# Attention values as products with tokens stationary and 512 weight columns moving

## Chip, cores and metric

The kernel runs on one core of a Trainium2 chip. The metric is the device time of one execution in microseconds (us). The engines are TensorE (PE, with its weight loads shown apart as PEld), VectorE (DVE), ScalarE (ACT), GpSimd (POOL) and SyncE (SP); each works through its own instructions in the order of the program, and DMA transfers are started from the queues of SP and POOL. In this kernel SP starts the loads of weights, and POOL starts the loads of attention's tables and the stores of keys and values.

## The reference, cut to what matters

Two layers of a block work on 128 context tokens and 256 latent tokens. Of one layer, what the change touches is this:

```
u = h @ w_in
u_pool, u_q, u_k, u_v, u_x, u_y, u_g = jnp.split(u, SPLITS, axis=-1)
q = u_q.reshape(b, l, N_HEADS, HEAD_DIM)
k = u_k.reshape(b, l, N_HEADS, HEAD_DIM)
v = u_v.reshape(b, l, N_HEADS, HEAD_DIM)
y_b = attn_fn(q, k, v).reshape(b, l, ATTN_W)
...
s_lat = einsum('brqhd,brkhd->bhrqk', qg, kb) * ATTN_SCALE + bias
s_ctx = einsum('brqhd,bkhd->bhrqk', qg, ck) * ATTN_SCALE
p = softmax(concatenate([s_lat, s_ctx], axis=-1), axis=-1)
o = einsum('bhrqk,brkhd->brqhd', p_lat, vb) + einsum('bhrqk,bkhd->brqhd', p_ctx, cv)
```

The width of h is 1024; there are 8 heads of 64, so u_v is 512 wide. The values v of the context tokens are also an output of the kernel (new_cache_v). Attention mixes tokens, so it needs v with tokens on the partitions, while everything else in the kernel has features on the partitions and tokens in the free dimension.

## The kernel before

All 384 tokens go through the layer together. A product of the main stream is a job (the function of that name): a chunk of weights, 8 blocks of 128 by 128, is stationary, the 384 tokens move, and each block takes three matmuls, since weights and data are split into an exact high and a low half (`whi`, `wlo`; `hh`, `hl`; L341 to L343). So a job of one chunk is 24 matmuls into one bank of PSUM. The order of the chunks is written out in chunk_order; SP loads them ahead, ACT makes the high half (L304) and DVE the low half (L313).

Other work stands beside the main stream. After the matmuls of a job the program traces, in this order: one step of each evacuation that is under way (tick), one step of each side branch (side_step), the evacuation of the job itself (push), and some steps of modulation on DVE (after). The side branches are Python generators; what a step traces goes to the engines' programs at that place, so the order of the engines' work follows the order of the jobs.

The part that the change touches begins behind the gates of the recurrent branch. Two side branches are then started: branch_lru_scan, whose steps scan one chunk of channels in one direction on DVE (L655) and copy one column of state to `st` on POOL (L656), and branch_attn. The main stream goes through four pairs of heads; for each pair p, qkv(p) traces

- load_attn: four DMAs on POOL for the tables `bias` of the two heads (L679) and one for `ckv`, the cached keys and values of the pair (L682);
- a job for q, one for k and one for v of the pair; each is copied from PSUM by ACT (L857), and k and v go out by a DMA on POOL (L859).

branch_attn works in steps i = 0, 1, 2 and so on, one at each side_step, and starts with pair p once `v` of that pair is there. Step 4p begins the pair (begin): PE transposes three blocks of v (L764), which ACT copies back to SBUF as `vv` a step later (L796), and DVE adds the mask to the two bias tables (L688). Then the scores of the pair's first query tile follow on PE (L701): q is stationary, and k and the cached keys in `ckv` move. Later steps take the softmax, transpose the probabilities (L743) and multiply them with `vv` and `ckv` (L778, L783).

After the twelve jobs the main stream goes on with the gates and projections of branch 2 (the recurrent one), 16 jobs with a step of attention at each, and then of branch 1 (attention's own), before which all side work must have been traced.

Of the kernel before, what the change touches and what calls it, by code (L numbers as in the profile page):

```python
# [16 lines left out]
L = 2  # L17
# [28 lines left out]
# products that warm the tensor engine up, around the first modulation vectors  # L46
WN = (8, 1, 1)
# modulation steps for each group of products, by part of the layer
# [3 lines left out]
def chunk_order():  # L52
    o = []
    for l in range(L):
        ms = [0, 1, 2, 3, 16, 17, 18, 19, 20, 21, 22, 23]
        if l == 0:
            ms = [m for m in ms if m not in FIRST0]
        o += [("in", l, m, 8) for m in ms]
        o += [("pw", l, 0, 4)]
        for b in (0, 2, 1):  # L60
            o += [("in", l, 24 + b * 8, 8)]
            for d in range(8):
                if b == 0 and d in (2, 6):
                    o += [("lru", l, d // 4, 8)]
                if d < 7:
                    o += [("in", l, 25 + b * 8 + d, 8)]
                o += [("br", l, b * 8 + d, 4)]
            if b == 0:
                for p in range(4):
                    o += [("in", l, 4 + p, 8), ("in", l, 8 + p, 8), ("in", l, 12 + p, 8)]  # L70
        o += [("wo", l, d, 8) for d in range(8)]
        for i in range(KF):
            o += [("fi", l, 2 * i, 8), ("fi", l, 2 * i + 1, 8)]
        for d in range(8):
            o += [("fo", l, 3 * d, 8), ("fo", l, 3 * d + 1, 8), ("fo", l, 3 * d + 2, 6)]
    return o
# [13 lines left out]
def emit(ctx, tc, A, outs):  # L90
# [33 lines left out]
    # silu(c), features on partitions, as the stationary side of small products  # L124
# [13 lines left out]
    # sel[p, s] = 1 where p = s modulo 32  # L138
# [3 lines left out]
    # 2h / count at the clipped ends of the pooling windows  # L142
    edge = cp.tile([128, 4, 2, 8], F32, name="edge")

    # additive mask of key columns, last column first
    cmask = cp.tile([128, 64], F32, name="cmask")

    def build_consts():
        ti = small("ti")
        G.iota(ti, pattern=[[1, 8]], base=0, channel_multiplier=0, allow_small_or_imprecise_dtypes=True)  # L150
        for g in range(4):
            h = float(1 << g)
            V.tensor_scalar(edge[:, g, 0], ti, h, None, op0=OP.add)
            V.tensor_scalar(edge[:, g, 1], ti, -1.0, 2 * h - 1, op0=OP.mult, op1=OP.add)
            yield
        V.tensor_scalar(edge[:, :, 1], edge[:, :, 1], 1.0, None, op0=OP.max)
        yield
        V.reciprocal(edge, edge)
        yield
        for g in range(4):  # L160
            V.tensor_scalar(edge[:, g], edge[:, g], 2.0 * (1 << g), None, op0=OP.mult)
            yield
        G.memset(cmask, 0.0)
        for rr in range(2):
            v = cmask[rr * 64:(rr + 1) * 64]
            # query column p, key column c = 63 - i: c >= min(p - 8, 48) and c < max(p - 8, 0) + 16
            G.affine_select(v[:, 16:64], v[:, 16:64], pattern=[[-1, 48]], base=55,
                            channel_multiplier=-1, compare_op=OP.is_ge, fill=NEG)
            G.affine_select(v[:, 0:48], v[:, 0:48], pattern=[[1, 48]], base=-56,
                            channel_multiplier=1, compare_op=OP.is_ge, fill=NEG)  # L170

    # derived per-channel parameters, both layers at once
# [3 lines left out]
    def build_dpar():  # L176
# [5 lines left out]
        # -log_sigmoid(lam) = max(-lam, 0) + log1p(z), z = exp(-|lam|)  # L182
# [13 lines left out]
        # log1p(z) = 2 atanh(z / (2 + z)), s <= 1/3  # L196
# [28 lines left out]
    def load_crow():  # L225
        # silu(c) * 2, broadcast over partitions
        Q.dma_start(out=crow, in_=A["crow"].unsqueeze(0).to_broadcast([128, 2, D]))
# [102 lines left out]
    def w_ahead(done, full=False):  # L330
        """traced before the products with the last `done` chunks, which still hold their tiles"""
        n = ws["use"] + NH - done
        w_lo(min(ws["cv"], n))
        w_hi(n)
        if full or done > 2:
            w_lo(n if full or done > 3 else n - 1)
        w_dma(min(n + NR, ws["lo"] + NR))
# [7 lines left out]
    def split_from(src, n=NT, scale=1.0, name="s"):  # L345
        """float32 data in SBUF or PSUM (times scale) -> two float32r tiles"""
        hi, lo = heap(name + "h", F32R), heap(name + "l", F32R)
        S.activation(hi[:, :n], src, AF.Copy, scale=scale)
        if isinstance(scale, float) and scale == 1.0:
            V.tensor_tensor(lo[:, :n], src, hi[:, :n].bitcast(F32), op=OP.subtract)  # L350
        else:
            V.scalar_tensor_tensor(lo[:, :n], src, scale, hi[:, :n].bitcast(F32), op0=OP.mult, op1=OP.subtract)
        return hi, lo

    def split_g(put, src, n=NT, scale=1.0, name="s"):
        """split_from in two stages"""
# [50 lines left out]
    def job(mems, mv, evac, units=1.0, full=False):  # L407
        """mems: lists of chunks, one PSUM bank for each; k outermost where there are several"""
# [25 lines left out]
    def prep_x(l, which, d, shift=True):  # L434
        """x * g (1 + sc), not yet divided by the token's rms, with the shift as two more columns"""
# [56 lines left out]
    def normed(l, which, R, mv):  # L492
        """hi and lo of h = rmsnorm(x) * g * (1 + sc) + sh, a pair of tiles per block of features"""
# [36 lines left out]
    def first_group(l, which, keys, evs, kst):  # L530
        """the first products behind a norm: from x before the division, which the evacuation makes up for"""
# [22 lines left out]
    def seg_copy(dst, offs, src):  # L554
        """PSUM (or the pair that undo gives) to the two token ranges of a padded tile"""
# [7 lines left out]
    def branch_pool(l, g, up, y):  # L563
        h = 1 << g
        st = heap("ws")
        # sliding sum over [t - h, t + h)
# [36 lines left out]
    def lru_gates(l, c, w, y):  # L603
        """one chunk of channels, both directions"""
        q = dpar[l]
        xc, mv = y.pop(("xc", c))
        for e in range(2):
# [4 lines left out]
            def ev(pa, px, i, e):  # L612
# [5 lines left out]
                # log a = C (1 + th)  # L618
# [4 lines left out]
                V.scalar_tensor_tensor(t2[:, n], th[:, n], 1.0, t2[:, n], op0=OP.add, op1=OP.mult)       # 1 - a  # L623
                V.scalar_tensor_tensor(th[:, n], t2[:, n], 2.0, t2[:, n], op0=OP.subtract, op1=OP.mult)  # a^2 - 1
                yield
                S.activation(t2[:, n], t2[:, n], AF.Identity, scale=-1.0, bias=1.0)                      # a
# [43 lines left out]
    def load_attn(l, y, p):  # L670
        for h in (2 * p, 2 * p + 1):
            t = heap("bias")
            rpb = A["rpb"]
            for rr in range(2):
                lo = 5 - rr
                # the table's last axis comes reversed; key columns are laid out from the last to the first
# [13 lines left out]
    def branch_attn(l, y):  # L690
        def scores(p, qt):
            """both heads of a pair side by side, each on its half of the rows"""
# [64 lines left out]
        pr, o, tv, pend = {}, {}, {}, []  # L757
        nu = len(units)

        def begin(p):  # L760
            tp = psum("tp")
            vt = y["v", p]
            for j in range(3):
                T.transpose(tp[:, j * 128:(j + 1) * 128], vt[:, j * 128:(j + 1) * 128], ident)  # L764
            tv[p] = tp
            mask_bias(y, p)
# [20 lines left out]
        while i < nu + 7 or pend:  # L787
            if i < nu and ("v", units[i][0]) not in y:
                yield
                continue  # L790
# [3 lines left out]
            for p in list(tv):  # L794
                vv = heap("vv")
                S.activation(vv[:, :384], tv.pop(p)[:, :384], AF.Copy)  # L796
                y["vv", p] = vv
# [18 lines left out]
            if i % 4 == 2 and 0 <= i - 10 < nu:  # L816
# [3 lines left out]
                for key in (("vv", p), ("ckv", p), ("bias", 2 * p), ("bias", 2 * p + 1), ("q", p), ("k", p), ("v", p)):  # L820
                    y.pop(key)
# [32 lines left out]
    def ev_qkv(l, kind, p, y):  # L854
# [8 lines left out]
        return f  # L863

# [66 lines left out]
    def start(y):  # L931
        """modulation of the first norm on the tensor engine, beside the first products; its shift comes last"""
# [27 lines left out]
        def first_mod():  # L960
            """the first scales, one block of features at a time"""
# [76 lines left out]
        def warm(n):  # L1038
            """products of no use that keep the tensor engine's clock up while the first data comes"""
# [126 lines left out]
    for l in range(L):  # L1166
# [14 lines left out]
        def qkv(p):  # L1181
# [3 lines left out]
            win(12 + p, ev_qkv(l, "v", p, y))  # L1185
# [7 lines left out]
        for bi, b in enumerate((0, 2, 1)):  # L1193
# [17 lines left out]
            if b == 0:  # L1211
# [7 lines left out]
                modr[0] = MR[l][3]  # L1219
                for p in range(4):  # L1220
                    qkv(p)
# [31 lines left out]
    # the last norm, tokens on partitions  # L1253
# [24 lines left out]
def layout(i):  # L1278
# [7 lines left out]
    def fm(a):  # [..., n*128] -> [128, ...*n]  # L1286
# [13 lines left out]
    def tiles(w):  # [L, K, M] -> [L, M/128, 128(k), K/128, 128(m)]  # L1300
# [4 lines left out]
    # the first products and their modulation, in the order of their use  # L1305
# [3 lines left out]
    A["in0"] = c(w0.transpose(3, 0, 2, 1, 4).reshape(8, 2, 128, 384))  # L1309
    A["pw"] = c(f["pool_w"].transpose(0, 2, 1, 3).reshape(L, 1, 128, 4, 128))  # L1310
# [40 lines left out]
```

## Time and profile before

| | |
|---|---|
| median of 3 runs | 1251.04 us |
| lowest and highest of the runs | 1250.4 and 1251.63 us |
| span of the profiled execution (its own time, from the first to the last instruction) | 1250.2 us |
| PE busy, share of the span | 99% |
| DVE, ACT, POOL busy, share of the span | 71%, 48%, 6% |

The span is that of one execution that the profiler took; the runs are timed without it, and their median is 0.84 us above this span. A view of the trace gives, for an engine, what it did and when, and what ended the idle time before it.

### The profile page before, as it was taken

The numbers are of one execution on the slowest core, as the hardware profiler recorded it, in microseconds if no ns is written. First come the engines' busy times: TensorE is split into PE (matmuls) and PEld (weight loads), VectorE is DVE, ScalarE is ACT, GpSimd is POOL, SyncE is SP. The second block draws the span as 40 slices with busy tenths as digits, with TensorE's granted clock in tenths as the row PEclk, the third lists the DMA queues.
The fourth block names the chain that finished last, engine by engine and source line by source line (L and its number), as shares of the span: only waits on it lengthen the run. The fifth ranks groups of instructions, "written<-read, shape, count | busy, mean of one in ns | idle before, by whom it ended". The sixth has DMA issues, their size and how long they took to land.

```text
span 1250.2 us, 19496 instructions
## 1 busy us (share of the span) xinstructions
PE 1237.8 (99%) x7414; PEld 1213.4 (97%) x7414; DVE 888.6 (71%) x1650; ACT 599.8 (48%) x1095; POOL 73.0 (6%) x187
## 2 busy tenths in 40 slices
PE   8999999999999999999999999999999999999997
PEld 7799999999999999999999999999999999999997
DVE  5788798988977987756779668975676784442432
ACT  4487765534456333333347577553344743332331
POOL 0000141000200000010000013200010000000000
PEclk8999999999999999999999999999999999999999
DMA  9646676456645666646643557733554365333421
GB/s 330 239 127 211 173 146 155 142 188 209 208 129 172 237 229 206 208 137 191 210 147 103 159 168 171 143 111 118 169 186 135 116 205 168 132 108 103 121 78 51
DMA packets 65438, 204.32 MB, mean 163 GB/s; under 512 B 7744, under 2 KB 12992, under 8 KB 65216
## 3 DMA queue, kind: packets, MB, share of 16 engines
q1 hardware_dynamic: 62848, 197.82, 48.6%
q0 software_dynamic: 2496, 5.25, 4.0%
q8 instruction: 58, 0.95, 0.3%
q14 instruction: 36, 0.29, 0.1%
HBM read 200.41 MB, written 2.63 MB: 162 GB/s over the span
## 4 chain that ended last, share of the span: by engine, by line
PE 73%; issue 22%; DVE 3%; ACT 1%; DMA 0%; SPq 0%; POOLq 0%; POOL 0%; DVEq 0%
PE ps L341 23%; PE ps L343 22%; PE ps L342 22%; PE tp L743 1%; PE sc L701 1%; PE o L783 1%; DVE wlo L313 1%; PE ma L954 1%; DMA w<-in_wm 0%; PE fb L1144 0%; DVE hf L655 0%; ACT th L634 0%; DVE ti L648 0%; PE o L778 0%; ACT whi L304 0%
## 5 line engine op out<-in xcount | busy, mean ns | idle before, releaser
L341 PE MATMUL ps<-hh,whi 128*128 128x384 f32 x1320 | 447.3, 339 | 0.0
L343 PE MATMUL ps<-hl,whi 128*128 128x384 f32 x1320 | 444.5, 337 | 0.0
L342 PE MATMUL ps<-hh,wlo 128*128 128x384 f32 x1320 | 444.3, 337 | 0.0
L313 DVE TENSOR_TENSOR wlo<-raw,whi 128x1024 fp32r<-128x1024 f32 (+2 forms) x296 | 322.4, 1114 | 22.8 <-ACT whi L304 22.8
L304 ACT ACTIVATE whi<-raw 128x1024 fp32r<-128x1024 f32 (+2 forms) x296 | 280.1, 970 | 102.9 <-PE ps L343 62.0
L341 PEld LDWEIGHTS ps<-hh,whi 128*128 128x128 f32 x1320 | 247.8, 188 | 1.6 <-issue 0.3
L343 PEld LDWEIGHTS ps<-hl,whi 128*128 128x128 f32 x1320 | 247.8, 188 | 0.0
L342 PEld LDWEIGHTS ps<-hh,wlo 128*128 128x128 f32 x1320 | 247.8, 188 | 0.0
L261 DVE SCALAR_TENSOR_TENSOR junk<-wm,crow 128x1024 bf16<-128x1024 f32 x160 | 195.2, 1220 | 26.3 <-DMA wm<-in_wm 24.2
L343 PE MATMUL ps<-svl,whi 128*128 128x384 f32 x352 | 118.7, 337 | 0.0
L341 PE MATMUL ps<-svh,whi 128*128 128x384 f32 x352 | 118.6, 337 | 0.0
L905 ACT ACTIVATE ft<-ps 128x384 f32<-128x384 f32 x40 | 19.7, 492 | 206.0 <-PE ps L343 206.0
L342 PE MATMUL ps<-svh,wlo 128*128 128x384 f32 x352 | 118.3, 336 | 0.0
L890 DVE SCALAR_TENSOR_TENSOR x<-ps,modv,x 128x128 f32<-128x128 f32 x64 | 23.7, 411 | 85.2 <-PE ps L343 85.0
L907 DVE TENSOR_TENSOR ft<-ft,ps 128x384 f32<-128x384 f32 x40 | 22.0, 551 | 84.2 <-ACT ft L905 66.7
L868 ACT ACTIVATE tg<-ps 128x384 f32<-128x384 f32 x48 | 23.5, 489 | 114.5 <-PE ps L343 114.5
L343 PEld LDWEIGHTS ps<-svl,whi 128*128 128x128 f32 x352 | 66.1, 188 | 0.0
L341 PEld LDWEIGHTS ps<-svh,whi 128*128 128x128 f32 x352 | 66.1, 188 | 0.0
L342 PEld LDWEIGHTS ps<-svh,wlo 128*128 128x128 f32 x352 | 66.1, 188 | 0.0
L877 DVE SCALAR_TENSOR_TENSOR tg<-tg,ps 128x384 f32<-128x384 f32 x48 | 26.5, 551 | 53.5 <-PE ps L343 53.0
L452 ACT ACTIVATE sq<-x 128x384 f32<-128x384 f32 x40 | 20.1, 513 | 67.4 <-DVE x L890 67.4
L342 PE MATMUL ps<-mgh,wlo 128*128 128x384 f32 x128 | 43.2, 338 | 0.0
(239 smaller groups left out, 1713.0 us busy)
## 6 DMA issues: line engine op xcount, KB each, us to landing
raw<-in_in SPq DMA_DIRECT2D x90, 512.0 KB, 4.2
raw<-in_fi SPq DMA_DIRECT2D x88, 512.0 KB, 4.3
wm<-in_wm SPq DMA_DIRECT2D x80, 512.0 KB, 4.6
raw<-in_fo SPq DMA_DIRECT2D x32, 512.0 KB, 4.6
raw<-in_br SPq DMA_DIRECT2D x48, 256.0 KB, 2.9
w<-in_wm SPq DMA_DIRECT2D x16, 512.0 KB, 7.0
raw<-in_wo SPq DMA_DIRECT2D x16, 512.0 KB, 4.2
raw<-in_fo SPq DMA_DIRECT2D x16, 384.0 KB, 3.2
```

Source lines behind the costliest of these rows:

```text
L261: V.scalar_tensor_tensor(j, t, 0.5, crow[:, s], op0=OP.mult, op1=OP.mult, accum_out=modv[l][:, comp, d, s:s + 1])
L304: S.activation(hi[:, :nk], r[:, :nk], AF.Copy)
L313: V.tensor_tensor(lo[:, :nk], r[:, :nk], hi[:, :nk].bitcast(F32), op=OP.subtract)
L341: T.matmul(ps[:, :n], hi[:, k], mv[0][:, :n], start=start, stop=False)
L342: T.matmul(ps[:, :n], lo[:, k], mv[0][:, :n], start=False, stop=False)
L343: T.matmul(ps[:, :n], hi[:, k], mv[1][:, :n], start=False, stop=stop)
L452: S.activation(sq[:, :NT], xt[d], AF.Square)
L868: S.activation(t[:, :NT], ps[:, :NT], AF.Tanh, scale=0.5)
L877: V.scalar_tensor_tensor(t[:, :NT], t[:, :NT], 1.0, ps[:, :NT], op0=OP.add, op1=OP.mult)
L890: V.scalar_tensor_tensor(xt[d][:, o:o + n], ps[:, o:o + n], modv[l][:, comp, d, s:s + 1], xt[d][:, o:o + n], op0=OP.mult, op1=OP.add)
L905: S.activation(t[:, :NT], pg[:, :NT], AF.Silu)
L907: V.tensor_tensor(t[:, :NT], t[:, :NT], pu[:, :NT], op=OP.mult)
```

## The change

The values of all eight heads are computed in one go ahead of the pairs, by values_job. The 128 by 128 blocks of the tokens (`hh`, `hl`) are now stationary, 512 columns of weights move, and the result comes out with tokens on the partitions: three banks of PSUM (`vt`), one for each 128 tokens, all 512 value columns in each. The weights come in four chunks of the same 128 by 1024 size, laid out as two blocks of features by 512 columns. After each chunk one tick, one side_step and one after are traced, as behind a job. ev_values copies the banks to `vv` on ACT, a bank at each of three ticks, in pieces of 128 columns, and stores the context tokens' values from `vv`. The v job of each pair, the transposes of v and the copies of the transposes are gone. The layout of the output in memory follows. Comments were removed as well, so line numbers differ by a few.

```
             if b == 0:
+                o += [("vw", l, j, 8) for j in range(4)]
                 for p in range(4):
-                    o += [("in", l, 4 + p, 8), ("in", l, 8 + p, 8), ("in", l, 12 + p, 8)]
+                    o += [("in", l, 4 + p, 8), ("in", l, 8 + p, 8)]
...
         def begin(p):
-            tp = psum("tp")
-            vt = y["v", p]
-            for j in range(3):
-                T.transpose(tp[:, j * 128:(j + 1) * 128], vt[:, j * 128:(j + 1) * 128], ident)
-            tv[p] = tp
             mask_bias(y, p)
...
-            if i < nu and ("v", units[i][0]) not in y:
+            if i < nu and ("k", units[i][0]) not in y:
                 yield
                 continue
...
-            for p in list(tv):
-                vv = heap("vv")
-                S.activation(vv[:, :384], tv.pop(p)[:, :384], AF.Copy)
-                y["vv", p] = vv
...
+    def ev_values(l, y, pss):
+        vv = [heap("vv") for _ in range(4)]
+        for t in range(3):
+            for p in range(4):
+                S.activation(vv[p][:, 128 * t:128 * t + 128], pss[t][:, 128 * p:128 * p + 128], AF.Copy)
+                if t == 0:
+                    G.dma_start(out=outs["v"][l, p], in_=vv[p][:, 0:128])
+                else:
+                    y["vv", p] = vv[p]
+            if t < 2:
+                yield
...
             win(8 + p, ev_qkv(l, "k", p, y))
-            win(12 + p, ev_qkv(l, "v", p, y))
+
+        def values_job():
+
+            pss = [psum("vt") for _ in range(3)]
+            for j in range(4):
+                hi, lo = [t.rearrange("p (a b) m -> p a (b m)", a=2) for t in w_get("vw", l, j)]
+                w_ahead(1)
+                for kk in range(2):
+                    k = 2 * j + kk
+                    for t in range(3):
+                        xh, xl = [m[:, 128 * t:128 * t + 128] for m in mv[k]]
+                        T.matmul(pss[t], xh, hi[:, kk], start=k == 0, stop=False)
+                        T.matmul(pss[t], xl, hi[:, kk], start=False, stop=False)
+                        T.matmul(pss[t], xh, lo[:, kk], start=False, stop=k == KD - 1)
+                tick()
+                side_step()
+                after()
+            push(ev_values(l, y, pss))
...
                 modr[0] = MR[l][3]
+                values_job()
                 for p in range(4):
                     qkv(p)
...
+    wv = f["w_in"][:, :, 1536:2048].reshape(L, 4, 2, 128, 512)
+    A["vw"] = c(wv.transpose(0, 1, 3, 2, 4).reshape(L, 4, 128, 8, 128))
```

Where this moves instructions shows best on POOL, at the start of attention in the first layer. Before, POOL's program stands like this there (`bias` and `ckv` are the loads of a pair, `st` the copies of the scan's state, `out_k` and `out_v` the stores):

```order
L840 MEMSET xp 128x2 x9
L679 DMA bias<-in_rpb 64x6x64 x4
L682 DMA ckv<-in_ckv 128x256
L656 COPY st_1915<-hf 128x1
L859 DMA out_k<-k 128x128
L656 COPY st_1915<-hf 128x1
L859 DMA out_v<-v 128x128
L679 DMA bias<-in_rpb 64x6x64 x4
L682 DMA ckv<-in_ckv 128x256
```

After the change the same place of POOL's program reads:

```order
L832 MEMSET xp 128x2 x9
L657 COPY st_1894<-hf 128x1 x3
L863 DMA out_v<-vv 128x128 x4
L680 DMA bias<-in_rpb 64x6x64 x4
L683 DMA ckv<-in_ckv 128x256
L657 COPY st_1894<-hf 128x1 x2
L851 DMA out_k<-k 128x128
```

The loads of the first pair stood ahead of all of this; they now stand behind three copies of the scan's state and behind the four stores of the values.

On PE, at the first scores of the same layer, before (`tp` are the transposes of v, `sc` the scores):

```order
L342 MATMUL ps<-hh,wlo 128x384
L343 MATMUL ps<-hl,whi 128x384
L764 MATMUL tp<-ident,v 128x128 x3
L701 MATMUL sc<-k,q 128x256 x2
L701 MATMUL sc<-ckv,q 128x128 x2
L701 MATMUL sc<-k,q 128x128 x2
L341 MATMUL ps<-hh,whi 128x384
```

and after:

```order
L343 MATMUL ps<-hh,wlo 128x384
L344 MATMUL ps<-hl,whi 128x384
L702 MATMUL sc<-k,q 128x256 x2
L702 MATMUL sc<-ckv,q 128x128 x2
L702 MATMUL sc<-k,q 128x128 x2
L342 MATMUL ps<-hh,whi 128x384
L343 MATMUL ps<-hh,wlo 128x384
```

The transposes are gone, and these scores now stand behind the 72 matmuls of the values and three jobs (q and k of the first pair, q of the second), where they stood behind four jobs.

On ACT, from the square roots of the scan branch on (`th`), before:

```order
L634 ACTIVATE th<-th 128x386 x8
L857 ACTIVATE q<-ps 128x384
L304 ACTIVATE whi<-raw 128x1024
L857 ACTIVATE k<-ps 128x384
L304 ACTIVATE whi<-raw 128x1024
L857 ACTIVATE v<-ps 128x384
L304 ACTIVATE whi<-raw 128x1024
L358 ACTIVATE ych<-hf 128x384
```

and after:

```order
L635 ACTIVATE th<-th 128x386 x8
L305 ACTIVATE whi<-raw 128x1024 x3
L359 ACTIVATE ych<-hf 128x384
L861 ACTIVATE vv<-vt 128x128 x4
L305 ACTIVATE whi<-raw 128x1024
L861 ACTIVATE vv<-vt 128x128 x4
L849 ACTIVATE q<-ps 128x384
L305 ACTIVATE whi<-raw 128x1024
L861 ACTIVATE vv<-vt 128x128 x4
```

The first four copies to `vv`, for which the four stores on POOL wait, stand behind `ych`, the high half of the first scanned chunk.

## Rows read from the trace of the kernel before

**Rows 1.** The page: span, busy time of the engines, chain that ended last.

```profile
span 1250.2 us, 19496 instructions
...
PE 1237.8 (99%) x7414; PEld 1213.4 (97%) x7414; DVE 888.6 (71%) x1650; ACT 599.8 (48%) x1095; POOL 73.0 (6%) x187
...
PE 73%; issue 22%; DVE 3%; ACT 1%; DMA 0%; SPq 0%; POOLq 0%; POOL 0%; DVEq 0%
```

**Rows 2.** Waits of PE: who waited for whom, total, times, longest.

```profile
PE ma L966 <- DMA w<-in_wm: 3.0, 2, 1.9
PE warm L1042 <- POOL ident masks.py:199: 1.4, 1, 1.4
```

**Rows 3.** Timeline of PE, first layer: start, length, instruction, count.

```profile
146.15 0.34 PE L341 MATMUL ps<-hh,whi 128*128 128x384 f32 x1
...
162.82 0.34 PE L343 MATMUL ps<-hl,whi 128*128 128x384 f32 x1
162.99 0.49 PE L764 MATMUL tp<-ident,v 128*128 128x128 f32 x3
163.41 0.70 PE L701 MATMUL sc<-k,q 64*128 64x256 f32 x4
163.95 0.39 PE L701 MATMUL sc<-ckv,q 64*128 64x128 f32 x4
...
172.83 0.34 PE L343 MATMUL ps<-hl,whi 128*128 128x384 f32 x1
173.10 0.70 PE L701 MATMUL sc<-k,q 64*128 64x256 f32 x4
```

**Rows 4.** The same of the second layer, first product of its q, k, v.

```profile
748.88 0.34 PE L341 MATMUL ps<-hh,whi 128*128 128x384 f32 x1
```

**Rows 5.** A stretch near the start: busy PE, PEld, DVE, ACT, POOL; granted clock, DMA.

```profile
8.80:15.70 6.90, 6.19 (x34) 5.77 (x35) 3.04 (x13) 2.08 (x7) 0.00 (x0) 0.51 1.06 392
```

**Rows 6.** Timeline of PE at the start of the program.

```profile
9.51 1.08 PE L966 MATMUL ma<-w,sA 128*32 128x128 f32 x16 [1.85 <-DMA w<-in_wm]
...
12.08 0.52 PE L341 MATMUL ps<-xsh,w0h 128*128 128x384 f32 x1
12.40 0.52 PE L342 MATMUL ps<-xsh,w0l 128*128 128x384 f32 x1
```

**Rows 7.** ACT by line and shape: count, busy time, mean ns of one.

```profile
L709 ACT ACTIVATE pr<-sc 128x128 f32<-128x128 f32 x32 | 8.7, 271 | 0.1
...
L857 ACT ACTIVATE v<-ps 128x384 f32<-128x384 f32 x8 | 3.9, 483 | 4.3 <-PE ps L343 4.3
```

**Rows 8.** Timeline of POOL, first layer.

```profile
143.45 2.80 POOL L679 DMA_DIRECT2D bias<-in_rpb  x4 [80.10 <-PE ps L343]
...
161.39 0.54 POOL L859 DMA_DIRECT2D out_v<-v  x1
161.93 2.63 POOL L679 DMA_DIRECT2D bias<-in_rpb  x4
...
165.79 0.56 POOL L656 COPY st<-hf 128x1 f32<-128x1 f32 x1 [0.67 <-DVE hf L655]
```

**Rows 9.** Timeline of DVE: third scan, in the first and the second layer.

```profile
165.30 0.42 DVE L655 TENSOR_TENSOR_SCAN hf<-t,ti 128x128 f32<-128x128 f32 x1
...
766.89 0.43 DVE L655 TENSOR_TENSOR_SCAN hf<-t,ti 128x128 f32<-128x128 f32 x1
```

**Rows 10.** Timeline of ACT, first layer, at the first scanned chunk.

```profile
164.89 0.53 ACT L358 ACTIVATE ych<-hf 128x384 fp32r<-128x384 f32 x1 [3.60 <-DVE hf L662]
```

**Rows 11.** From issue to landing, shortest, median, longest: `ckv` (8 loads), then `out_v` (8 stores).

```profile
DMA to landing us min/median/max: 7.4/9.1/10.2
...
DMA to landing us min/median/max: 1.8/2.4/4.5
```

**Rows 12.** Stretches of attention, first layer: PE, PEld, DVE, ACT, POOL busy.

```profile
163.00:196.80 33.80, 33.46 (x211) 31.68 (x210) 32.08 (x71) 16.94 (x41) 15.03 (x25) 1.00 0.74 130
196.80:264.00 67.20, 67.20 (x478) 62.46 (x478) 60.15 (x151) 37.06 (x98) 1.08 (x2) 1.00 0.54 162
```

More of the change, by code (lines that the diff above doesn't have):

```diff
@@ L756, in branch_attn @@
         units = [(p, hh, qt) for p in range(4) for qt in range(2) for hh in range(2)]
-        pr, o, tv, pend = {}, {}, {}, []
+        pr, o, pend = {}, {}, []
         nu = len(units)
         def begin(p):
-            tp = psum("tp")
-            vt = y["v", p]
-            for j in range(3):
-                T.transpose(tp[:, j * 128:(j + 1) * 128], vt[:, j * 128:(j + 1) * 128], ident)
-            tv[p] = tp
             mask_bias(y, p)
@@ L819, in branch_attn @@
                 next(pend[-1])
-                for key in (("vv", p), ("ckv", p), ("bias", 2 * p), ("bias", 2 * p + 1), ("q", p), ("k", p), ("v", p)):
+                for key in (("vv", p), ("ckv", p), ("bias", 2 * p), ("bias", 2 * p + 1), ("q", p), ("k", p)):
                     y.pop(key)
@@ L1346 @@
     k = np.asarray(R["out_k"]).reshape(L, 512, 128).transpose(0, 2, 1).reshape(1, L, 128, 8, 64)
-    v = np.asarray(R["out_v"]).reshape(L, 512, 128).transpose(0, 2, 1).reshape(1, L, 128, 8, 64)
+    v = np.asarray(R["out_v"]).reshape(L, 4, 128, 128).transpose(0, 2, 1, 3).reshape(1, L, 128, 8, 64)
     s = np.asarray(R["out_s"]).reshape(L, 128, 4, 2).transpose(0, 3, 2, 1).reshape(1, L, 2, 512)
```

## The prediction

> **What bounds the kernel now.** I read the page first: the span is 1250.2 us, PE is busy for 99% of it, DVE for 71%, ACT for 48%, POOL for 6% [rows 1]. Then the waits of PE: the two largest entries, 3.0 and 1.4 us, both belong to the start of the program, and what follows them is tenths [rows 2]. So PE sets the time by the length of its own program, and two things can change it: how long PE's instructions take, and a wait that PE does not have today. The timeline of PE gives the stage. In the first layer q, k and v begin at 146.15; four jobs later, at 162.99, the transposes of v follow, the first scores at 163.41 and those against `ckv` at 163.95 [rows 3]. In the second layer the stage begins at 748.88 [rows 4].
>
> **The values on PE.** Four jobs are 96 matmuls of 384 columns in 162.99 − 146.15 = 16.84 us, 175.4 ns each; a job of 24 is 4.21 us [rows 3]. The change takes away four of these jobs per layer, 192 matmuls in both, 33.7 us, and adds 2 × 72 = 144 matmuls of 512 columns. No row shows a matmul of 512. The nearest are those of 384 columns at the two clock levels. Near the start the granted clock is 0.51, about 1.2 GHz [rows 5], and there two such matmuls start 320 ns apart [rows 6]; at the full clock it is 175. The difference, 145 ns, is what halving the clock adds, so some 145 ns of the 175 go with the columns and 30 do not: 512 columns give 145 × 4/3 + 30 = 223 ns. If all of it goes with the columns, it is 175.4 × 4/3 = 234 ns. I take 228 between them, since the rows don't tell which: 144 × 0.228 = 32.8 us, a change of **−0.7 us** (−1.6 to 0).
>
> The Trainium skill, page "TensorE: Matmul & The Clock Gate", section "Back-to-back issue gap", gives N/2.4 + 2.5 ns for the spacing at the full clock; as an estimate, that is 216 ns at 512 columns and would make this term −2.6 us. The row at 384 columns shows 175 ns where that rule gives 162.5, so I stay with the rows.
>
> **The transposes.** From 162.99 to 163.41 three transposes take 0.42 us; the scores that stood behind them will instead stand behind a job. Where a score stands behind a job today, it starts 0.27 us after the last matmul (172.83 to 173.10), while the transposes start 0.17 after it (162.82 to 162.99) [rows 3]. So a group costs 0.42 + 0.17 − 0.27 = 0.32 us, and the eight groups of both layers **−2.6 us**.
>
> **ACT.** Per layer, four copies of v and four of the transposes go, 0.483 us each (the row of v counts 8 for both layers; the copies of the transposes have its shape), 3.9 us; twelve pieces of 128 columns come, at 0.271 by the nearest copy of that size, 3.3 us [rows 7]. ACT is busy 48% of the time, so this costs and gives nothing, so long as no order of PE or POOL hangs on it; the first four pieces do, see below. The weights' bytes are the same. Where PE starts a job a few us earlier or later, the loads on SP's queue stand ahead of it as before; I book nothing.
>
> **POOL: what is late next.** POOL works in order. Today the loads of the first pair (`bias` four times, then `ckv`) are issued from 143.45 on, after 80 us in which POOL had nothing to do [rows 8], about 17 us ahead of the scores. In the new order they stand behind three copies of scan state and four stores of values. The third copy waits for the third scan of DVE. That scan starts at 165.30 [rows 9] and its copy runs from 165.79 to 166.35 [rows 8]. The scans stay at their slots (one after each chunk of values, 18 × 0.228 = 4.1 us, in place of one after each job, 4.2), so I keep this time. The stores wait for the copies to `vv`, and these stand on ACT behind `ych`, 164.89 + 0.53 [rows 10]; four copies more end at 166.5, so they hold POOL up little. Then: 166.35 + 4 stores × 0.54 = 168.5; four `bias` loads, 2.63 [rows 8]; so `ckv` is issued at **171.1**. From its issue to its landing such a load takes 7.4 to 10.2 us, 9.1 in the median [rows 11]: it lands at **180.2** (178.5 to 181.3).
>
> PE gets there earlier: 146.15 + 72 × 0.228 + three jobs (q and k of pair 0, q of pair 1) × 4.21 + 0.54 from the first score to the first against `ckv` = **175.7**. So PE waits 4.5 us (2.8 to 5.6). Behind those scores on PE stands the whole main stream, so nothing hides it. DVE waits too, for `bias`, whose issue ends just ahead of `ckv`'s. Behind the mask on DVE stand scans and the low halves of weights; in this stretch DVE is busy 32.08 of 33.80 us, and 60.15 of 67.20 in the next [rows 12], so it makes up little of a delay; but its delay falls while PE stands too, so I add none.
>
> In the second layer the scan starts at 766.89 [rows 9]; with the same 1.05 us to the end of its copy, 767.9 + 2.16 + 2.63 = 772.7 for the issue and 781.8 for the landing. PE is there at 748.88 + 16.4 + 12.6 + 0.54 = 778.5. It waits 3.3 us (1.6 to 4.4). The four stores are now ahead of the loads in the queue as well; by the spread of the loads above their median, 1.1 us [rows 11], that is 0 to 1.1 for each layer, and I take 0.3. **All waits: 4.5 + 3.3 + 0.6 = +8.4 us.** Later pairs have a pair's time more, and I see no wait there.
>
> **The clock.** Today PE has no gap inside the layers. At the start, where it waited 1.85 us for weights [rows 6], the granted clock fell to 0.51 until 15.70 [rows 5]. From 12.08 on, PE works densely: 3.6 us hold 11 matmuls of 320 ns, each 145 ns too long, 1.6 us. The bounds per wait are 0 (no fall) and 3.1 (a whole stretch of 6.9 us dense, 21.6 matmuls). As part of a low stretch can fall into the wait itself, where it costs nothing, I take two thirds of 1.6, 1.1, for each of two waits: **+2.2 us.**
>
> **Sum.** −0.7 − 2.6 + 8.4 + 2.2 = +7.3 on the profiled 1250.2 us; the median of the runs is 0.84 above that span, so 1258.3 us, slower.
>
> **The rivals.** (1) *The wait, but no fall of the clock*: 7.3 − 2.2 = +5.1, 1256.1 us. For it: the wait is one gap of 3 to 5 us in hundreds of dense us, unlike the sparse start; against it: the only gaps of this length in the trace go with a low clock.
> (2) *Short waits*: both loads land in the shortest time, 7.4 us, and the clock stays: 2.8 + 1.6 − 3.3 = +1.1, 1252.1 us, no change that can be told (a measurement of this kernel tells some 0.2%, 2.5 us, from no change). For it: spread of a landing is 2.8 us; against it: both would have to be the quickest.
> (3) *No wait, faster*: −3.3, 1247.7 us. It decides where `ckv` lands within 175.7 − 171.1 = 4.6 us of its issue (5.8 in the second layer), or where it is issued some 4 us earlier. For it: the stores of values, on the same queue, land in 1.8 to 4.5 us [rows 11], so a transfer can be that quick. Against it: no load of `ckv` was quicker than 7.4.
> The Trainium skill, page "DMA: Bandwidth & Descriptors", section "Anatomy of one DMA — SWDGE (gpsimd) path", speaks for (3): 2.0 us plus bytes over 436 GB/s, as an estimate 2.3 us for these 128 KB, so no wait at all. The trace does not agree: 7.4 to 10.2.
> (4) *More*: the longest landings (5.6 + 4.4), the 0.6, the clock at 1.6 for each and 512 columns at 234 ns: 0 − 2.6 + 10.6 + 3.2 = +11.2, 1262.2 us, or beyond if DVE, 90% busy in the 67 us behind [rows 12], can't catch up and PE waits for it again.
> (5) *The matmuls gain nothing*: 512 columns at 234 ns. That is +0.7 on the forecast, 1259.0, and is counted with it.
>
> **How the numbers follow.** The forecast with (5) 0.51, (1) 0.22, (2) 0.11, (3) 0.12, (4) 0.04. Only (3) is faster by over 0.2%, with a small part of (2): 0.13. The rest of (2) is the same: 0.10. Slower: 0.77. The range from 1250.2 to 1263.2 leaves (3) and the far part of (4) out, under 2 in 10; its low end takes in short waits with the values at −1.6. Without (3) and (2), slower cases alone lie from 1254 to 1263.
>
> **What the profile after would show.** Among the waits of PE, the scores against `ckv` twice, for a DMA, 4 to 5 and 3 to 4 us, near 176 and 779; POOL issuing `ckv` near 171 and 773; DVE idle ahead of the mask until `bias` lands; a granted clock below 1.00 in the us behind each wait; matmuls into `vt` 223 to 234 ns apart; no transposes of v. I am wrong if `ckv` is issued early enough after all (copies or stores sooner than counted), if it lands in under 5 us, or if a wait that I don't see (weights, banks of PSUM, DVE) comes first.

## The result

The changed kernel takes 1258.89 us in the median of 4 runs (1258.22 to 1259.17), the kernel before 1251.31 in the runs beside it: a ratio of 1.0058, with a 95% interval of 1.0046 to 1.0071. It is slower by 7.6 us; 1258.3 were forecast, in a range from 1250.2 to 1263.2. A repeat on another occasion gave 1.0052 (1.0038 to 1.0066).

The page after, to be read beside [rows 1]:

```profile
span 1257.3 us, 19371 instructions
...
PE 1237.9 (98%) x7342; PEld 1206.5 (96%) x7342; DVE 889.4 (71%) x1650; ACT 598.5 (48%) x1103; POOL 71.7 (6%) x187
...
PE 69%; issue 23%; DVE 3%; ACT 2%; DMA 2%; POOL 1%; SPq 0%; POOLq 0%; DVEq 0%; ACTq 0%
```

The span grew by 7.1 us and PE is busy as long as before, 1237.9 against 1237.8 us, with 72 matmuls fewer. So the growth is time in which PE stands, and DMA and POOL have come into the chain that ended last. The waits of PE (total, times, longest) say what for; [rows 2] is what they were:

```profile
PE sc L702 <- DMA ckv<-in_ckv: 6.6, 2, 4.3
PE ma L970 <- DMA w<-in_wm: 3.2, 2, 2.4
...
PE tp L744 <- DVE pr L735: 0.5, 1, 0.5
```

One entry is new: two waits for `ckv`, 4.3 and 2.2 us, one in each layer. The timeline of POOL, first in the first layer, shows why `ckv` is late, beside [rows 8], where the same loads began at 143.45:

```profile
165.09 0.56 POOL L657 COPY st<-hf 128x1 f32<-128x1 f32 x1 [4.33 <-DVE hf L656]
165.59 2.34 POOL L863 DMA_DIRECT2D out_v<-vv  x4
167.92 2.62 POOL L680 DMA_DIRECT2D bias<-in_rpb  x4
170.52 0.59 POOL L683 DMA_DIRECT2D ckv<-in_ckv  x1
...
772.80 0.56 POOL L657 COPY st<-hf 128x1 f32<-128x1 f32 x1 [3.19 <-DVE hf L656]
773.30 2.21 POOL L863 DMA_DIRECT2D out_v<-vv  x4
775.50 2.61 POOL L680 DMA_DIRECT2D bias<-in_rpb  x4
778.10 0.58 POOL L683 DMA_DIRECT2D ckv<-in_ckv  x1
```

The copy waits for DVE's scan, and stores and loads stand behind it, one after the other. The timeline of PE shows what follows, beside [rows 3, 4]:

```profile
145.84 0.39 PE L1200 MATMUL vt<-whi,hh 128*128 128x512 f32 x1
...
162.50 0.34 PE L342 MATMUL ps<-hh,whi 128*128 128x384 f32 x1
...
175.22 0.70 PE L702 MATMUL sc<-k,q 64*128 64x256 f32 x4
180.26 0.80 PE L702 MATMUL sc<-ckv,q 64*128 64x128 f32 x4 [4.33 <-DMA ckv<-in_ckv]
180.85 0.64 PE L702 MATMUL sc<-k,q 64*128 64x128 f32 x4
181.42 0.69 PE L342 MATMUL ps<-hh,whi 128*128 128x384 f32 x1
181.90 0.52 PE L343 MATMUL ps<-hh,wlo 128*128 128x384 f32 x1
182.22 0.52 PE L344 MATMUL ps<-hl,whi 128*128 128x384 f32 x1
...
185.42 0.39 PE L342 MATMUL ps<-hh,whi 128*128 128x384 f32 x1
185.65 0.34 PE L343 MATMUL ps<-hh,wlo 128*128 128x384 f32 x1
...
754.68 0.40 PE L1200 MATMUL vt<-whi,hh 128*128 128x512 f32 x1
...
771.36 0.33 PE L342 MATMUL ps<-hh,whi 128*128 128x384 f32 x1
...
784.09 0.70 PE L702 MATMUL sc<-k,q 64*128 64x256 f32 x4
787.02 0.49 PE L702 MATMUL sc<-ckv,q 64*128 64x128 f32 x4 [2.23 <-DMA ckv<-in_ckv]
787.35 0.39 PE L702 MATMUL sc<-k,q 64*128 64x128 f32 x4
787.67 0.44 PE L342 MATMUL ps<-hh,whi 128*128 128x384 f32 x1
787.95 0.33 PE L343 MATMUL ps<-hh,wlo 128*128 128x384 f32 x1
```

The first scores start at 175.22, those against `ckv` at 180.26, 5.04 us later where it was 0.54 before [rows 3]. From 181.42 to 185.42 twelve matmuls run that start 0.32 us apart once they are under way (181.90 to 182.22); then the spacing is that of before again. In the second layer the same distance is 2.93 us (784.09 to 787.02), and no slow matmul follows the wait. The stretches behind the two waits (busy PE, PEld, DVE, ACT, POOL, granted clock) agree, beside [rows 5]:

```profile
180.26:185.42 5.16, 5.16 (x20) 4.94 (x21) 5.09 (x10) 0.85 (x3) 0.56 (x1) 0.50 0.48 147
787.02:791.00 3.98, 3.98 (x27) 3.86 (x28) 3.91 (x8) 0.86 (x3) 0.53 (x1) 1.00 0.84 234
```

At 0.50, about 1.2 GHz, PE is "busy" all through the first stretch and starts a matmul every 0.32 us in place of 0.175; its busy time alone would not show this.

### The profile page after: what moved, and what is told of

Its sections match the earlier page's. It is cut to its first block, busy times and chain, and to the rows that moved or that the text cites. A ratio compares the mean times of both kernels' runs of the same rounds, so it can differ in the third digit from the quotient of the medians.

```text
span 1257.3 us, 19371 instructions
## 1 busy us (share of the span) xinstructions
PE 1237.9 (98%) x7342; PEld 1206.5 (96%) x7342; DVE 889.4 (71%) x1650; ACT 598.5 (48%) x1103; POOL 71.7 (6%) x187
## 4 chain that ended last, share of the span: by engine, by line
PE 69%; issue 23%; DVE 3%; ACT 2%; DMA 2%; POOL 1%; SPq 0%; POOLq 0%; DVEq 0%; ACTq 0%
PE ps L342 22%; PE ps L344 21%; PE ps L343 21%; DMA ckv<-in_ckv 1%; PE sc L702 1%; PE tp L744 1%; PE o L779 1%; DVE wlo L314 1%; DVE junk L262 1%; PE ma L958 1%; ACT whi L305 1%; DMA w<-in_wm 0%; PE fb L1148 0%; ACT th L635 0%; POOL bias L680 0%
## 5 line engine op out<-in xcount | busy, mean ns | idle before, releaser
L342 PE MATMUL ps<-hh,whi 128*128 128x384 f32 x1256 | 426.5, 340 | 0.0
L343 PE MATMUL ps<-hh,wlo 128*128 128x384 f32 x1256 | 423.9, 338 | 0.0
L344 PE MATMUL ps<-hl,whi 128*128 128x384 f32 x1256 | 423.6, 337 | 0.0
L342 PEld LDWEIGHTS ps<-hh,whi 128*128 128x128 f32 x1256 | 236.4, 188 | 2.5 <-issue 0.6
L343 PEld LDWEIGHTS ps<-hh,wlo 128*128 128x128 f32 x1256 | 236.3, 188 | 0.1
L344 PEld LDWEIGHTS ps<-hl,whi 128*128 128x128 f32 x1256 | 236.4, 188 | 0.0
L872 ACT ACTIVATE tg<-ps 128x384 f32<-128x384 f32 x48 | 23.4, 488 | 90.6 <-PE ps L344 89.8
L342 PE MATMUL ps<-mgh,whi 128*128 128x384 f32 x128 | 43.2, 338 | 0.0
```

The source lines that it names most:

```text
L342: T.matmul(ps[:, :n], hi[:, k], mv[0][:, :n], start=start, stop=False)
L343: T.matmul(ps[:, :n], lo[:, k], mv[0][:, :n], start=False, stop=False)
L344: T.matmul(ps[:, :n], hi[:, k], mv[1][:, :n], start=False, stop=stop)
L872: S.activation(t[:, :NT], ps[:, :NT], AF.Tanh, scale=0.5)
```

## The experiments

The theory (A): the loss is the late loads of the first pair alone, by PE's waits and by the clock that they pull down; the new products by themselves are a small gain. The rival (B): the loss belongs to the new products or to attention that begins three jobs later (DVE is late, another load is next), and the wait for `ckv` only stands where something else would wait anyway. Two questions lie inside A: what makes a load land 9 us after its issue, and whether it is the gap that lowers the clock. The times of before beside each run were 1251.0 to 1251.6 us; ratios are compared below.

### The loads first again

```
+                load_attn(l, y, 0)
                 values_job()
                 for p in range(4):
                     qkv(p)
```

and within qkv the call of load_attn stands only for the later pairs.

> The changed kernel with the loads of the first pair issued ahead of the values, where they stood before the change; nothing else differs. Theory A, the loss is the late loads alone: both waits of PE for ckv and the stretch of low clock go (4.3 + 2.2 + about 2.3 us), what stays is the gain on PE: transposes -2.6 and values -0.4 (512 columns measured 231 ns apart) on 1251.3, so 1248.3 us, 0.2% under the kernel before. Theory B, attention that begins three jobs later is a loss by itself (DVE or another load is late next): PE waits for something else near the first scores and the time stays at 1251 to 1254 us.

Measured: 1249.21 us, ratio 0.9982 (0.9973 to 0.9991). POOL issues `ckv` at 146.44, and the waits of PE hold no `ckv` any more:

```profile
PE ma L970 <- DMA w<-in_wm: 2.4, 1, 2.4
...
PE tp L744 <- DVE pr L735: 0.5, 1, 0.5
```

This is A. One call moved ahead of the values turns the change from 0.58% slower to 0.18% faster, and the waits show nothing else that is late next (what the dots stand for, 1.4 and 0.7 us, belongs to the start of the program). Of the 3.0 us that A forecast as gain, 2.4 came; the interval (1.1 to 3.4 us) leaves room for a cost of attention's later start of up to 2 us, which the waits do not show. By its median this is the fastest of all the versions; the one below with `ckv` ahead lies within its interval.

### The late loads alone, in the kernel before

```
             if i < nu and ("v", units[i][0]) not in y:
+                n_wait += 1
+                if n_wait == 2:
+                    load_attn(l, y, 0)
                 yield
```

Here too load_attn stands in qkv for the later pairs only.

> The kernel before, with its own products of the values and its transposes, but with the loads of the first pair issued one copy of scan state later, near 156 in place of 143 us. It adds the late loads alone. Theory A: ckv is issued near 158.5 and lands 7 to 9 us later, at 166 to 167.5; PE comes at 163.95 and waits 2 to 3.4 us, in both layers; with 0 to 2.2 us of low clock for each wait 1251.6 + 4 to 11, some 1258 us, slower by 0.5%, without any of the change's products. Theory B, the loss belongs to the new products or to attention's later start: 1251.6 us, no change.

Measured: 1265.31 us, ratio 1.0112 (1.0097 to 1.0128), 14 us slower. From POOL's and PE's timelines and the waits of PE:

```profile
156.02 2.81 POOL L679 DMA_DIRECT2D bias<-in_rpb  x4
158.81 0.60 POOL L682 DMA_DIRECT2D ckv<-in_ckv  x1
```

```profile
168.12 0.49 PE L701 MATMUL sc<-ckv,q 64*128 64x128 f32 x4 [4.12 <-DMA ckv<-in_ckv]
...
777.78 0.80 PE L701 MATMUL sc<-ckv,q 64*128 64x128 f32 x4 [5.29 <-DMA ckv<-in_ckv]
```

The issue came where it was expected, the landing later: 9.3 us after the issue in the first layer (158.81 to 168.1) and 10.6 in the second (767.15 to 777.8), so the waits are 4.1 and 5.3 us in place of 2 to 3.4, and I had sized them too small. Behind each, 11 and 13 matmuls run 0.32 us apart. 9.4 us of waits and 24 × 0.145 = 3.5 us of low clock make 12.9 of the 13.5 us by which the span grew (1263.7 against 1250.2). So the late loads make such a loss, and a larger one, without any of the change's products; together with the version before this one, B falls.

### The stores of the values behind the loads

```
-                if t == 0:
-                    G.dma_start(out=outs["v"][l, p], in_=vv[p][:, 0:128])
-                else:
+                if t:
                     y["vv", p] = vv[p]
...
+        for p in range(4):
+            G.dma_start(out=outs["v"][l, p], in_=vv[p][:, 0:128])
```

> The changed kernel with the four stores of values issued after the last copy to vv, behind the first pair's loads; the loads still stand behind three copies of scan state. Theory A: the loads are issued some 2.3 us earlier (four stores of 0.54) and land as much earlier; the wait of the first layer falls from 4.3 to about 2.0, that of the second from 2.2 to 0, and at a wait of 2 us the clock stays up, as it did in the second layer: 1258.9 - 2.3 - 2.2 - 2.3 = 1252.1 us. Theory B: 1258.9 us, no change.

Measured: 1254.87 us, ratio 1.0026 (1.0017 to 1.0035). About half the loss goes, but less than expected; two of the ten runs took 1252.2 us, where theory A put it, the other eight 1254.07 to 1255.70, and the trace is of one of the eight, so why these two were faster is not shown. The waits of PE for `ckv`, and a stretch behind the first (columns as above):

```profile
PE sc L702 <- DMA ckv<-in_ckv: 4.0, 2, 2.4
```

```profile
177.60:181.30 3.70, 3.67 (x16) 3.45 (x17) 3.67 (x7) 0.00 (x0) 3.01 (x5) 0.54 1.03 129
```

The first wait shrank as expected, by 1.9 us, the second only from 2.2 to 1.6, and the clock fell to 0.54 behind a wait of 2.4 us, where I had expected it to stay up. From the third copy of the scan's state to the issue of `ckv` it is 2.1 us less in both layers (3.3 and 3.2 us in place of 5.4 and 5.3); in the second layer the load then took 10.3 us to land in place of 8.9, so less of this arrived. So the stores account for some 2.1 us of issue time; what is left of the waits goes once the loads stand ahead of the copies too, as the first version shows.

### ckv ahead of the bias tables

```
     def load_attn(l, y, p):
+        t = heap("ckv")
+        G.dma_start(out=t[:, :256].rearrange("p (a c) -> p a c", a=2), in_=A["ckv"][l, p])
+        y["ckv", p] = t
         for h in (2 * p, 2 * p + 1):
...
-        t = heap("ckv")
-        G.dma_start(out=t[:, :256].rearrange("p (a c) -> p a c", a=2), in_=A["ckv"][l, p])
-        y["ckv", p] = t
```

> The changed kernel with ckv loaded ahead of the four bias tables of each pair, in place of behind them. Theory A1, the 9 us from issue to landing are mostly the queue working off the four bias loads ahead (they land 1 to 2 us apart): ckv lands 2 to 5 us after its issue near 168, before PE comes at 175.8; PE does not wait, DVE waits for bias about a us longer: 1250.0 us. Theory A2, such a load takes 7 to 10 us by itself: it lands near 177.6, PE waits 1.8 us in the first layer and not in the second: 1252 us. Theory B, DVE's wait for bias is what costs: 1258 us or more.

Measured: 1249.87 us, ratio 0.9986 (0.9977 to 0.9995). The time from issue to landing (shortest, median, longest of the 8 loads of `ckv`), first in this kernel, then in the changed one, beside [rows 11]:

```profile
DMA to landing us min/median/max: 2.3/4.0/8.4
```

```profile
DMA to landing us min/median/max: 5.1/9.3/13.3
```

The load of the first pair in the first layer alone, in the same order (size, us from issue to landing):

```profile
ckv<-in_ckv POOLq DMA_DIRECT2D x1, 128.0 KB, 3.3
```

```profile
ckv<-in_ckv POOLq DMA_DIRECT2D x1, 128.0 KB, 9.7
```

In the second layer it is 3.6 against 8.9. PE's scores against `ckv` follow without a wait, while DVE still stands for the tables:

```profile
174.42 0.70 PE L702 MATMUL sc<-k,q 64*128 64x256 f32 x4
174.96 0.39 PE L702 MATMUL sc<-ckv,q 64*128 64x128 f32 x4
```

```profile
175.96 0.56 DVE L689 TENSOR_TENSOR bias<-bias,cmask 128x384 f32<-128x384 f32 x1 [1.03 <-DMA bias<-in_rpb]
179.31 0.56 DVE L689 TENSOR_TENSOR bias<-bias,cmask 128x384 f32<-128x384 f32 x1 [2.79 <-DMA bias<-in_rpb]
```

So the 9 us of [rows 11] were not what such a transfer takes: most of them are the four bias loads ahead of it in the queue. They are issued within 2.6 us, but the two tables that they fill are ready 3.4 us apart (the masks at 175.96 and 179.31). The Trainium skill, page "DMA: Bandwidth & Descriptors", section "Anatomy of one DMA — SWDGE (gpsimd) path", gives 2.0 us plus the bytes over 436 GB/s, as an estimate 2.3 us for these 128 KB. The trace of before did not bear this out (7.4 to 10.2 us); here the shortest of the eight loads agrees, 2.3 us, and their median of 4.0 does not. The longest, 8.4 us, was issued at 195.25 while a table of the pair before was still on its way (it landed 11.5 us after its issue at 187.9). DVE's stand of 3.8 us while PE works comes back in part, as later waits of PE for DVE (0.5 us where the loads come first):

```profile
PE tp L744 <- DVE pr L735: 1.6, 2, 1.1
```

By these waits the late tables cost about a us; the times (1249.87 against 1249.21 us) do not tell the two versions apart, since the ratio of each lies inside the other's interval.

### Work in the wait, for the clock

```
             q, k, ck = y["q", p], y["k", p], y["ckv", p]
+            if l == 0 and p == 0 and qt == 0:
+                for _ in range(36):
+                    T.matmul(ss[0][:, 0:128], ident, ident, start=True, stop=True)
```

> The changed kernel with 36 additional products of 128 columns on PE ahead of the first scores of the first layer, into a place that the scores overwrite; about 3.9 us of work in the 4.3 us in which PE waits for ckv. It measures the clock's share. If the wait lowered the clock: PE stays near 1.00 behind it, and the time falls by what 12 matmuls at 320 in place of 175 ns and the slow scores cost, about 2.2 us, to 1256.7 us, though PE does more. If the low clock has another cause: 1258.9 us or a little more, with the low stretch still there.

Measured: 1261.16 us, ratio 1.0077 (1.0064 to 1.0091). The filling was too long: each such product runs as two matmuls, and the 36 took 8.2 us, not 3.9, so PE was no longer waiting when `ckv` landed, and its scores against `ckv` start at 183.77, not 180.26.

```profile
175.11 8.20 PE L698 MATMUL sc<-ident 128*128 128x128 f32 x72
```

The clock stayed up behind it, but the filling itself costs more than the clock gives back, so the time says nothing. The same with 17 products:

> As the first filling, with 17 additional products, since one took 0.226 us there and not 0.109: 3.84 us of work in the 4.3 us of the first layer's wait. If the clock falls only because PE stands still: the granted clock stays at 1.00, the 12 slow matmuls and the slow scores go, and the time falls by about 2.2 us to 1256.7 us, with ckv landing where it did. If the low clock has another cause: 1258.9 us.

Measured: 1257.88 us, ratio 1.0053 (1.0039 to 1.0066): the fall of 0.05% lies inside the intervals. In the first layer the clock was 1.00 from 180.40 on; but this time the second layer, which was not filled, went low behind a wait of 2.20 us, and by the spacing of its scores and matmuls took back some 1.4 of the 2.2 us that the first had gained:

```profile
180.40:186.00 5.60, 5.60 (x40) 5.46 (x37) 5.53 (x11) 1.27 (x5) 0.56 (x1) 1.00 0.54 150
...
784.50:787.80 3.30, 3.22 (x15) 3.00 (x16) 3.23 (x6) 0.65 (x3) 0.00 (x0) 0.51 0.83 197
```

So both layers were filled (17 products in the first, 8 in the second), with the changed kernel itself beside it:

```
+            if p == 0 and qt == 0:
+                for _ in range((17, 8)[l]):
+                    T.matmul(ss[0][:, 0:128], ident, ident, start=True, stop=True)
```

> The changed kernel once more, unchanged, beside the next run on the same chip, since what is to be told apart there is 0.2%: 1258.9 us, 0.58% above the kernel before.

> The changed kernel with 17 additional products ahead of the first scores in the first layer (3.84 us in a wait of 4.3) and 8 in the second (1.8 us in a wait of 2.2), so that neither layer has a gap over 0.7 us. If the gaps lower the clock: it stays at 1.00 behind both, nothing of the waits is won back, and the time is the changed kernel's without its low clock, 2.2 us less where that has it in the first layer alone: 1256.7 us, 0.4% above the kernel before. If the low clock has another cause, or costs nothing: the changed kernel's time.

Measured: the changed kernel 1258.34 us, ratio 1.0052 (1.0038 to 1.0066); with both gaps filled 1256.68 us, ratio 1.0039 (1.0026 to 1.0051), 1.7 us less, though PE has 25 × 0.226 = 5.7 us more to do. First the stretches behind the first scores with the filling, then those of the changed kernel beside it (its slow matmuls run from 179.86 to 183.1 and from 784.92 to 787.3, so the two stretches hold a part of them):

```profile
180.30:186.00 5.70, 5.69 (x37) 5.57 (x38) 5.60 (x10) 1.32 (x5) 0.56 (x1) 1.00 0.48 135
...
784.30:790.00 5.70, 5.70 (x37) 5.58 (x38) 5.56 (x13) 1.37 (x5) 0.56 (x1) 1.00 0.73 196
```

```profile
178.00:181.60 3.60, 3.60 (x20) 3.48 (x21) 3.57 (x7) 0.00 (x0) 0.00 (x0) 0.74 0.59 108
784.30:786.40 2.10, 2.10 (x13) 1.88 (x10) 2.06 (x4) 0.09 (x1) 0.00 (x0) 0.50 0.89 205
```

By the clock's rows it is shown that the gap lowers the clock and that work in it keeps it up: all three filled waits of the first layer stayed at 1.00, both unfilled ones of the changed kernel went low. The second layer alone would not show it, since unfilled it stayed up once. The intervals of the two ratios overlap, but all five runs with the filling (1255.47 to 1257.23) lie below all five of the changed kernel beside them (1257.5 to 1258.47), so the fall in time is clear too. Its size is less so: 2.2 us were expected, from the first trace of the changed kernel; in the trace beside this run the low clock costs about 3 us (17 slow matmuls × 0.145 = 2.5, and 0.5 for the scores of the second layer), and 1.7 were won.

### The transposes put back

With the loads first, three transposes of k for each pair, into a place that the scores overwrite:

```
             if qt == 0:
+                for j in range(3):
+                    T.transpose(ss[0][:, j * 128:j * 128 + 128], k[:, j * 128:j * 128 + 128], ident)
                 parts.append((slice(384, 512), k, slice(0, 128), 0))
```

> The changed kernel with the first pair's loads issued early, and in each pair three transposes of k on PE ahead of the first scores, into a place that the scores overwrite: it adds the transposes back without their use. By the forecast they cost 0.32 us a pair, 2.6 us in all: 1249.2 + 2.6 = 1251.8 us, as the kernel before, so that the transposes are nearly all that the change gains on PE. If PE hides them (weight loads beside products): 1249.2 us.

Measured: 1250.75 us, ratio 0.9998 (0.9989 to 1.0007), against 0.9982 without them. The difference, 0.16%, is 2.0 us; the intervals leave room for the 2.6 of the forecast. PE's timeline at the first group:

```profile
174.03 0.34 PE L344 MATMUL ps<-hl,whi 128*128 128x384 f32 x1
174.21 0.49 PE L699 MATMUL sc<-ident,k 128*128 128x128 f32 x3
174.62 0.70 PE L704 MATMUL sc<-k,q 64*128 64x256 f32 x4
```

With the transposes back, the kernel is as fast as before, within the interval: nearly all that the change gains on PE is that they are gone.

## Why the prediction was right

**The values on PE.** The 72 matmuls of 512 columns take 162.50 − 145.84 = 16.66 us and 771.36 − 754.68 = 16.68 us, 231.5 ns each, near the upper bound of 234: a column costs nearly the same at 512 as at 384 (0.452 and 0.457 ns). The term is 33.3 − 33.7 = −0.3 us, not −0.7; the forecast's own figures, 32.8 − 33.7, give −0.9, so there was a slip of 0.2 in it as well. The estimate from the Trainium skill, page "TensorE: Matmul & The Clock Gate", section "Back-to-back issue gap", 216 ns, does not agree with these rows.

**The transposes.** −2.6 was forecast, 2.0 measured by the times. On PE the first group costs what was forecast: 0.18 + 0.41 us (174.03 to 174.62) in place of the 0.27 from a job's last matmul to the scores, so 0.32. What came back may be a wait: with the loads first PE waits 0.5 us for `pr`, and with the transposes in place that entry is gone; but the kernel before has 0.3 us of it too, so this is not shown.

**The waits.** Issue at 171.1 was forecast and is 170.52, PE's coming at 175.7 and it is 175.8. From there to 180.26 it is 4.5 us, as forecast; the profile counts 4.3, from the modelled end of the scores ahead. That it fits so well is in part luck: the load was issued 0.6 us sooner and took 9.7 us in place of 9.1. In the second layer 3.3 were forecast, and 2.4 came (2.2 by the profile): there, PE's stage begins 5.8 us later in absolute time, but `ckv` was issued 23.4 us behind its start (754.68 to 778.10), not 23.8, landed in 8.9 us, not 9.1, and PE came 0.3 us later than counted. The 0.6 for a fuller queue can't be told from the spread of the landings (one load 0.6 above the median, one 0.2 below it). Together 6.9 (6.6 by the profile) in place of 8.4. The repeat had 3.3 and 2.1 by the profile.

**The clock.** 1.1 for each layer was forecast. In the profiled execution the first layer paid for twelve matmuls, 1.7 us, and 0.5 for the scores (180.26 to 181.42, against 787.02 to 787.67), and the second nothing; in the repeat both paid, about 1.5 us each. The mechanism was right, but the even split was not: a wait paid nothing, or between 1.4 and 2.5 us by the spacing of the scores and matmuls behind it, and which one pays differs between executions. That the first execution paid 2.2 in all, the sum of the forecast, is luck, and no run tests the two thirds by which it was sized.

By the traces the terms are −0.3 − 2.6 + 6.9 + 2.2 = +6.2, and the waits for `pr` and for `w` at the start hold 0.4 more than before; the span grew by 7.1, so 0.5 us stays without an owner, less than the 1.2 us between the runs of the kernel before. So the path was right (POOL's order, the late load, two waits of PE, the clock behind them) and is shown by the experiments; that the number fits to less than a us is in part luck, since the waits were 1.5 us too long, the gain on PE 0.4 too large, and 0.9 was not counted at all.

Of the rivals, the first (the wait without a low clock) is what the second layer did in one execution. What I held against it, that gaps of 3 to 5 us go with a low clock in the trace of before, rested on one gap of 1.85 us; that trace has none of 3 to 5. Against the third, no wait, I held that no load of `ckv` landed in under 7.4 us. It failed as I said, but the reason was wrong: I took the landing times for a property of the load. Most of them is the place in the queue, and with `ckv` ahead of the tables PE does not wait.

## What to carry to other kernels

A step that is moved ahead takes its place on every in-order queue: look for the loads that now stand behind its stores and behind whatever those stores wait for, and issue the loads before it. A measured time from issue to landing belongs to a place in a queue; what is ahead of the load there may be most of it, and the order of the loads is then worth as much as their issue time. On a kernel whose bound engine is busy 99% of the time, a gap costs more than itself when the granted clock falls behind it.

## What the runs showed of the hardware beyond that

Whether a gap of 2 us lowers the clock differs between executions. Behind the four waits of 3.3 to 5.3 us the granted clock fell each time, for 10 to 13 matmuls; of the shorter ones, 1.58 and 2.23 us left it at 1.00, while 2.09, 2.20, 2.39 and 2.52 lowered it for 5 to 11 matmuls. Nor does the fall always stand right behind the wait: in the changed kernel's first trace the first scores were slow already, while in its repeat PE had worked for 1.9 us at the old spacing (178.00 to 179.86) before its matmuls slowed down. The length alone does not tell; what else decides it stays open.
